# The cross-attention queries of a two-layer encoder: head 0's raw weights loaded with the first sum, later sums loaded later, two tiles for A22's loads

## The chip, the cores and the metric

One core of a Trainium2 chip runs the whole kernel. The metric is the device time of one execution in microseconds (us), as the median of several runs.

## The reference

A two-layer encoder over 512 positions of width 1024, all in float32. Each layer has a mixer (forgetting and differential attention in layer 0, an mLSTM in layer 1), a cross-attention on a memory of 256 positions, and a gated feed-forward net with a short convolution. Cut to what surrounds the change:

```python
x = x + mixed                       # mixer's output projection: mixed @ w_out
x = x + memory_cross_attention(rms_norm(x, xattn_norm[layer]), rms_norm(mem, mem_norm[layer]),
                               xattn_wq[layer], xattn_wkv[layer], xattn_wo[layer])
x = x + conv_ffn(rms_norm(x, ffn_norm[layer]), ffn_w_up[layer], ...)

def memory_cross_attention(xn, memn, wq, wkv, wo):
    q = split_heads(xn @ wq, XATTN_HEADS)        # 4 heads of 256
    k, v = jnp.split(memn @ wkv, 2, axis=-1)
    ...
    out = jnp.einsum('bhqm,bhmd->bhqd', p.astype(v.dtype), v)
    return merge_heads(out) @ wo
```

The change concerns `xn @ wq`, in both layers.

## The kernel before

Activations are kept transposed: `x[0]` to `x[7]` are eight tiles of 128 of the 1024 channels by 512 positions. A product in float32 is made of three in a faster format (`fp32r`): both operands are split into a high part (a cast on ScalarE, ACT, L285) and a low part (a subtraction on VectorE, DVE, L282), and `mm3` (L291 to L293) issues high by high, high by low and low by high on TensorE (PE).

**Queries by seven products.** The weights of one head of `wq` (1024 by 256) and `xn` are taken as 2 by 2 blocks, and `p_query` forms a head's queries with seven block products in place of eight (`p1`, `q2`, `p5`, `p6`, `q7`, `p3`, `p4`). Of the weights it needs, for each head h:
- `raw`, the first half A11, A12 as it lies in memory (1024 columns); its load is L1197.
- `sa`, sums of both halves: `sum_load` loads a pair of blocks on SyncE's queue (SP, L1165) and adds the second half by an accumulating DMA that GpSimd (POOL) issues (L1166). There are three `sa` buffers.
- `sb`, first S2 = part of `sa` + part of `raw` (L1221, DVE), then S4, made in place from S2 and `raw` (L1232).
- `ra`, A22, loaded by `rest_load` (L1171), in a single buffer: the next head's load is issued once the present one has been split.

Of the activations it needs `xh`, `xl` (the two parts of normalised x, even tiles for `p1`, odd ones for `q2`) and four "forms", combinations of x tiles that `form_steps` makes from pairs of them (ACT L1480, DVE L1486 to L1488, ACT cast L1489 into `kv0` to `kv3` and DVE's subtraction into `kv4` to `kv7`).

**The stage.** The mixer's output projection runs over eight blocks (one for each x tile) of 24 matmuls of 512 columns. Each block's result stays in a PSUM bank (`acc`) until DVE adds it to x (L619); then ACT makes `xh` (L603), DVE `xl` (L604), both add up squares for the norm (L597, L598), and two tiles at a time become a form. Two banks are in turn: block m+2 needs the bank that x m has left, so the block of x4 starts when x2 is out. Meanwhile heads 0 and 1 of the queries are begun with the x tiles that exist. After the projection the queries of heads 0 to 3, the keys' products and the softmax follow. Head 0's `seed` (L1207, ACT) copies p1's result, negated, into an accumulator, before the rest of the head's products.

**What sets the order.** `Plan` takes steps with a priority (`p1_`, `p5_`, ...) and dependencies and decides the order in which PE's work is written; the order on DVE, ACT, SP and POOL is set by a recording layer from the same steps. On each engine instructions then run strictly as they stand, and a load that waits on SP holds up the loads behind it. Tiles come from pools with a fixed number of buffers for a name; a new tile waits for the readers of the one whose buffer it takes. `opened` opens the pool `keys` once the mixer's tiles are done with, and loads sums 0, 1 and 2. `fn` of `xattn` opens the pool of the cross-attention (`mp`), with `pg`, a tile whose bytes belong to operands of the mixer's projection until that has ended.

Of the kernel before, what the change touches and what calls it, by code (L numbers as in the profile page):

```python
# [17 lines left out]
P = 128  # L18
# [218 lines left out]
class Builder:  # L237
# [887 lines left out]
    def p_forms(self, pl, layer, mix, used):  # L1125

        def opened():
            mix.close()
            self.kp = self.keys.enter_context(self.tc.tile_pool(name=f"keys{layer}", bufs=1, side="right", reuse_waits="tile"))
            self.forms, self.sums = [], {}  # L1130
            for tag, n, bufs in (("sa", 1024, 3), ("ra", 512, 1)):
                self.til(self.kp, tag, (P, n), bufs=bufs)
            self.kv = [self.til(self.kp, f"kv{i}", (P, 1024), F32R, bufs=1) for i in range(8)]
            for tag in ("s2", "a22", "s4"):
                self.til(self.kp, tag, (P, 1088), F32R, bufs=1)
            self.til(self.kp, "sb", bufs=2)
            self.pad(self.kp, 128)
            for h in range(3):
                self.sum_load(layer, h)

        def form(k):
            th, tl = self.kv[k], self.kv[4 + k]
            self.forms.append((th, tl))
            f, r = self.til(self.kp, "a22", (P, 1088), bufs=1), self.til(self.kp, "s4", (P, 1088), bufs=1)
            for fn in self.form_steps(k, "xat", layer, f[:, :1024].rearrange("p (a b) -> p a b", a=2), r[:, :1024], th, tl):
                fn[1]()

        last = pl.add(opened, 0, used, 100, order=[self.memnorm])
        for k in range(3):
            last = pl.add(  # L1150
                lambda k=k: form(k), 0, self.xdone[2 * k + 1], 100 + 2 * k + 2, order=[last], chain=(("A", 1.5), ("D", 1.4), ("A", 1.0), ("D", 1.2))
            )
        self.formed = [last]
        self.queries = []
        for h in range(2):
            self.queries.append(self.p_query(pl, layer, h, [last] + [q[1] for q in self.queries]))
            self.queries[h] = self.queries[h], next(self.queries[h])
        self.held = [q[1].st for q in self.queries]
# [8 lines left out]

    def rest_load(self, layer, h):

        self.rest = self.til(self.kp, "ra", bufs=1)  # L1170
        self.nc.sync.dma_start(self.rest[:], self.t["xq"][layer, 2 * h + 1][:, 512:])  # L1171

    def p_query(self, pl, layer, h, order):

        nc = self.nc
        tt_ = nc.vector.tensor_tensor
        st = {}
        a1, a2 = self.t["xq"][layer, 2 * h], self.t["xq"][layer, 2 * h + 1]
# [14 lines left out]
        less = lambda out, a, b: tt_(out=out, in0=a[:, :256], in1=b[:], op=ALU.subtract)  # L1193

        def p1():
            st["raw"] = self.til(self.wp, "raw", (P, 1024), bufs=3)
            nc.sync.dma_start(st["raw"][:], a1)  # L1197
            if h == 0:
                self.rest_load(layer, 0)
            st["f3"] = self.parts(OFF)  # L1200
            self.split(*st["f3"], st["raw"][:])
            st["X"] = self.bank("w")
            product(st["f3"], 0, X(0, 0), "X", True)
# [11 lines left out]
        def kept(n, bank):  # L1215
            st[n] = self.til(mp, "xe", (P, MEM), bufs=4)
            nc.scalar.copy(st[n][:], st[bank][:, :256])

        def p6():
            st["sb"] = self.til(self.kp, "sb", bufs=2)  # L1220
            tt_(out=st["sb"][:], in0=self.sums[h][:, 512:], in1=st["raw"][:, :512], op=ALU.add)  # L1221
            if h == 0:
                self.sum_load(layer, 3)
            wide("s2", st["sb"][:])
            product(st["s2"], 0, T2, "Y", False, range(4 - (h == 0)))

# [3 lines left out]

        def p3():
            tt_(out=st["sb"][:], in0=st["sb"][:], in1=st["raw"][:, 512:], op=ALU.add)  # L1232
            wide("s4", st["sb"][:])
            product(st["s4"], 0, X(1, 1), "R", False)

        def p4():
            wide("a22", self.rest[:])
            if h < 3:
                self.rest_load(layer, h + 1)
            product(st["a22"], 0, T4, "Y", False)  # L1240

        n = 1.42
# [15 lines left out]
        pl, mp, fin, ends = yield sd  # L1258
# [9 lines left out]
        u5 = pl.add(lambda: kept("u5", "R"), 0, [q5], p5_ + 0.5, take=("e",))  # L1268
        u2 = pl.add(lambda: kept("u2", "Y"), 0, [q6], p6_ + 0.5, take=("e",))
# [9 lines left out]
    def xattn(self, layer):  # L1279
        nc, t, tc = self.nc, self.t, self.tc  # L1280
        with tc.tile_pool(name=f"xa{layer}", bufs=1, reuse_waits="tile") as mp:
            self.mp = mp
            pl = Plan(self.plan, [st["banks"][0] for st in [*self.fills, *self.held]], s=2, w=0, e=4, q=2, pt=2, wt=1, hs=2)
# [1 line left out]
            for _ in range(2):  # L1285
                self.til(mp, "hs", (P, 1088))
            self.til(mp, "tmp", (P, MEM))
            self.pad(mp, 2048)
            self.pad(mp, 64)
            for tag in ("qh", "ql"):  # L1290
                self.til(mp, tag, (P, 1024), F32R)
# [1 line left out]
            self.til(mp, "pg", (P, 1088), F32R, bufs=1)  # L1293
            self.til(mp, "xe", (P, MEM), bufs=4)
            self.til(mp, "mx", dtype=F32R)

            def last():
                f, r = self.til(mp, "hs", (P, 1088)), self.til(mp, "hs", (P, 1088))
                self.forms.append((self.kv[3], self.kv[7]))
                for fn in self.form_steps(3, "xat", layer, two(f[:, :1024]), r[:, :1024], *self.forms[3]):  # L1300
                    fn[1]()
# [10 lines left out]
            qs, qe = [None] * 4, [None] * 4  # L1312
# [43 lines left out]
            for h in range(4):  # L1356
                p = 50 + 10 * h
                ke = []
                for m in (2 * h, 2 * h + 1):
# [7 lines left out]
                    if m < 2 * len(self.fills):  # L1367
                        st = self.fills[m // 2]
# [3 lines left out]
                                order=ke[-1:] if m % 2 else (),  # L1372
# [125 lines left out]
    def ffn_steps(self, layer, mp):  # L1498
# [1 line left out]


        nc, t = self.nc, self.t
        sc = Sched(raw=3, h=3, s2=1, s4=1, a22=1, sa=3, sb=2, ra=1, hs=2, c=1, dr=2, u2=1, u5=1, act=10, acc=2, y=2, s=2, w=2)
        add = sc.add
        tt = lambda n: 0.055 + 1.06e-3 * n
        act = lambda n: 0.1 + 0.83e-3 * n
# [11 lines left out]
        def joined(deps, prio, free):  # L1518
            return add("-", 0.0, None, deps, prio, (), free, 0.0)

        RAWS = {"raw": (self.wp, 1024, 3), "dr": (mp, 512, 2), "sa": (self.kp, 1024, 3), "sb": (self.kp, 512, 2), "ra": (self.kp, 512, 1)}

        def raw_tile(st, tag):
            pool, n, bufs = RAWS[tag]
            st[tag] = self.til(pool, tag, (P, n), bufs=bufs)
            return st[tag]
# [81 lines left out]
        act_ = lambda: tuple(self.til(mp, i, dtype=F32R, bufs=10) for i in ("ah", "al"))  # L1608
        self.pad(mp, 64)
        act_()  # L1610
        self.pad(mp, 192)
        formed = []
        hs2 = [mp.tile([P, 2, 514], F32, name=f"hs{layer}{i}") for i in range(2)]
        for h in hs2:
# [657 lines left out]
```

## Time and profile before

| | |
|---|---|
| median of 3 runs | 1472.54 us (1472.54 to 1472.64) |
| profiled execution | 1473.89 us, of which the span of the core's instructions 1471.8 us |
| PE busy | 1445.4 us, 98% of the span, 9019 matmuls |
| DVE, ACT, POOL busy | 1258.1, 931.1, 75.1 us |
| mean granted clock of PE | 0.998 |
| DMA | 190.23 MB in 1471.8 us, mean 129 GB/s |
| queries of layer 0, of layer 1 | about 220 to 312 us, 930 to 1020 us of the span |

Times on a row of a timeline are the start in us from the span's start, then the duration in us, engine, line, operation and operands; in brackets is how long the engine stood idle before it and what ended that. A row of the chain of waits is start, duration and what was done or waited for. A row of windows has, for a stretch of the span, each engine's busy time with its count of instructions, the granted clock (1.00 is full), the share of DMA engines' time and GB/s. A row of DMA issues ends with the us from issue to landing.

### The profile page before, as it was taken

What the parts mean: (1) busy time and instruction counts of PE and PEld (TensorE: products, weight loads), DVE (VectorE), ACT (ScalarE), POOL (GpSimd) and SP (SyncE); (2) the same over time, 40 slices, a digit from 0 to 9 for tenths busy, and PEclk for the clock granted to TensorE, in tenths of its full rate; (3) what the DMA queues carried; (4) which work ended last, traced back from release to release, by engine and by line L of the source; (5) the groups of instructions that cost most, each with busy time, mean ns of one, the idle gap of its engine ahead of it and who ended that gap; (6) DMA issues with size and microseconds to landing.
All of it is one profiled execution on the core that took longest, in us unless ns stands there. A gap on an engine that the chain in (4) does not pass through costs nothing.

```text
span 1471.8 us, 24027 instructions
## 1 busy us (share of the span) xinstructions
PE 1445.4 (98%) x9019; PEld 1281.5 (87%) x9019; DVE 1258.1 (85%) x2284; ACT 931.1 (63%) x1655; POOL 75.1 (5%) x116
## 2 busy tenths in 40 slices
PE   9999999899999999999999999999999999999998
PEld 7888787798889999999888888888988999999987
DVE  7789986866799999999778988796769999999974
ACT  7688665665677665666447665565656765656654
POOL 0001120000000000000000100000000000000000
PEclk9999999999999999999999999999999999999999
DMA  5222336452236665553223331746314566555322
GB/s 198 86 73 72 122 119 196 136 180 101 79 119 172 175 159 165 151 165 83 83 101 103 118 103 65 208 114 186 132 49 129 151 175 177 157 154 162 108 68 76
DMA packets 70627, 190.23 MB, mean 129 GB/s; under 512 B 7520, under 2 KB 7520, under 8 KB 70512
## 3 DMA queue, kind: packets, MB, share of 16 engines
q1 hardware_dynamic: 62304, 161.38, 32.4%
q0 software_dynamic: 7200, 26.22, 10.2%
q8 instruction: 70, 1.15, 0.3%
q10 hardware_dynamic: 1008, 1.12, 0.2%
q14 instruction: 45, 0.37, 0.1%
HBM read 186.56 MB, written 2.13 MB: 128 GB/s over the span
## 4 chain that ended last, share of the span: by engine, by line
PE 75%; DVE 14%; ACT 5%; issue 3%; DMA 3%; POOL 0%; SPq 0%; DVEq 0%; ACTq 0%; POOLq 0%
PE acc L291 13%; PE acc L292 13%; PE acc L293 13%; PE w L293 6%; PE w L291 6%; PE w L292 6%; PE s L293 3%; PE s L291 3%; PE s L292 3%; DVE wl L282 3%; PE acc L352 2%; PE acc L354 2%; PE acc L353 2%; DVE c L1656 1%; DMA raw<-in_xq_dram 1%
## 5 line engine op out<-in xcount | busy, mean ns | idle before, releaser
L282 DVE TENSOR_TENSOR wl<-raw,wh 128x1024 fp32r<-128x1024 f32 (+3 forms) x185 | 218.8, 1183 | 30.8 <-ACT wh L285 27.6
L291 PE MATMUL acc<-xh,wh 128*128 128x256 f32 (+1 forms) x624 | 206.9, 332 | 0.1
L293 PE MATMUL acc<-xh,wl 128*128 128x256 f32 (+1 forms) x624 | 205.8, 330 | 0.2 <-DVE wl L282 0.2
L292 PE MATMUL acc<-xl,wh 128*128 128x256 f32 (+1 forms) x624 | 205.6, 329 | 0.0
L285 ACT CAST wh<-raw 128x1024 fp32r<-128x1024 f32 (+1 forms) x127 | 130.8, 1034 | 87.7 <-PE acc L292 43.7
L1656 DVE SCALAR_TENSOR_TENSOR c<-hs,vec,c 128x512 f32<-128x512 f32 x176 | 128.6, 747 | 7.2 <-ACT c L1649 5.9
L291 PEld LDWEIGHTS acc<-xh,wh 128*128 128x128 f32 x624 | 117.2, 188 | 12.1 <-ACT v L1893 0.6
L293 PEld LDWEIGHTS acc<-xh,wl 128*128 128x128 f32 x624 | 117.2, 188 | 12.1 <-DVE wl L282 0.6
L292 PEld LDWEIGHTS acc<-xl,wh 128*128 128x128 f32 x624 | 117.2, 188 | 11.5
L293 PE MATMUL w<-ah,wl 128*128 128x512 f32 x304 | 119.1, 392 | 0.0
L292 PE MATMUL w<-al,wh 128*128 128x512 f32 x304 | 118.6, 390 | 0.0
L291 PE MATMUL w<-ah,wh 128*128 128x512 f32 x304 | 118.5, 390 | 0.0
L1649 ACT ACTIVATE c<-hs,vec 128x512 f32<-128x512 f32 x88 | 69.2, 813 | 13.2 <-DVE hs L1796 11.7
L282 DVE TENSOR_TENSOR s<-sb,s 128x512 fp32r<-128x512 f32 x100 | 68.6, 686 | 5.5 <-ACT s L285 5.5
L293 PEld LDWEIGHTS w<-ah,wl 128*128 128x128 f32 x304 | 57.1, 188 | 11.9
L282 DVE TENSOR_TENSOR wl<-sa,wh 128x1024 fp32r<-128x1024 f32 x50 | 61.1, 1221 | 5.6 <-ACT wh L1727 3.2
L292 PEld LDWEIGHTS w<-al,wh 128*128 128x128 f32 x304 | 57.1, 188 | 10.0
L1727 ACT CAST wh<-sa 128x1024 fp32r<-128x1024 f32 x42 | 44.1, 1049 | 34.3 <-PE w L292 26.4
L291 PEld LDWEIGHTS w<-ah,wh 128*128 128x128 f32 x304 | 57.1, 188 | 9.8
L619 DVE TENSOR_TENSOR x<-w,x 128x512 f32<-128x512 f32 x72 | 49.5, 688 | 18.1 <-PE w L293 18.0
L1545 ACT CAST wh<-dr 128x512 fp32r<-128x512 f32 x64 | 39.6, 618 | 39.2 <-issue 35.5
L1727 ACT CAST s<-sb 128x512 fp32r<-128x512 f32 x84 | 52.1, 620 | 18.5 <-PE s L293 14.6
(525 smaller groups left out, 4631.0 us busy)
## 6 DMA issues: line engine op xcount, KB each, us to landing
raw<-in_up_dram SPq DMA_DIRECT2D x46, 512.0 KB, 3.2
sa<-in_up_dram SPq DMA_DIRECT2D x42, 512.0 KB, 3.7
sa<-in_up_dram POOLq DMA_DIRECT2D x42, 512.0 KB, 5.2
dr<-in_down_dram SPq DMA_DIRECT2D x64, 256.0 KB, 2.9
ra<-in_up_dram SPq DMA_DIRECT2D x42, 256.0 KB, 3.2
raw<-in_xk_dram SPq DMA_DIRECT2D x16, 512.0 KB, 3.4
raw<-in_wo_dram SPq DMA_DIRECT2D x16, 512.0 KB, 3.3
raw<-in_xv_dram SPq DMA_DIRECT2D x16, 512.0 KB, 3.3
```

The costliest lines, as they stand in the source:

```text
L282: self.nc.vector.tensor_tensor(out=lo, in0=v, in1=hi.bitcast(F32), op=ALU.subtract)
L285: self.nc.scalar.copy(hi, v)
L291: mm(out, wh, xh, start=first, stop=False, skip_group_check=parts)
L292: mm(out, wh, xl, start=False, stop=False, skip_group_check=parts)
L293: mm(out, wl, xh, start=False, stop=last, skip_group_check=parts)
L352: mm(ps, xh[k][:, ts], wh[:, ws], start=(k == 0), stop=False)
L353: mm(ps, xh[k][:, ts], wl[:, ws], start=False, stop=False)
L619: self.nc.vector.tensor_tensor(out=self.x[m][:], in0=ps[:], in1=self.x[m][:], op=ALU.add)
L1545: nc.scalar.copy(st["wh"][:, :cols], st[tag][:, :cols])
L1649: nc.scalar.activation(st["c_"][:, j, :], hs()[:, j, 2:514], AF.Identity, scale=self.col("cw", (layer * 3 + 2) * 44 + blk), bias=self.col( ...
L1656: nc.vector.scalar_tensor_tensor(out=c, in0=hs()[:, j, n : n + 512], scalar=w, in1=c, op0=ALU.mult, op1=ALU.add)
L1727: nc.scalar.copy(s["wh"][:, :cols], raw())
```

## The change

Five edits, in both layers:
1. `ra` has two buffers; `rest_load` of head h+2 is issued after head h's A22 has been split (before: of head h+1).
2. `opened` loads sum 0, then head 0's raw weights, into the second of the three `sa` buffers (`self.first`), then head 0's A22. Sum 1 is a step of the plan just behind. Sum 2 is loaded in `p6` of head 0, sum 3 in `p3` of head 0; each takes an `sa` buffer that was read.
3. Head 2's raw weights go to `pg` instead of a `raw` buffer.
4. `sb` of heads 1 and 3 is a tile `qs` of the cross-attention's pool; a pad of 2048 bytes there goes.
5. The feed-forward stage has two `ra` buffers too, in its planner (`Sched`) and its table of tiles; a pad of 192 goes.

```diff
-            for tag, n, bufs in (("sa", 1024, 3), ("ra", 512, 1)):
+            for tag, n, bufs in (("sa", 1024, 3), ("ra", 512, 2)):
...
-            for h in range(3):
-                self.sum_load(layer, h)
+            self.rests = []
+            self.sum_load(layer, 0)
+            self.first = self.til(self.kp, "sa", (P, 1024), bufs=3)
+            self.nc.sync.dma_start(self.first[:], self.t["xq"][layer, 0])
+            self.rest_load(layer, 0)
...
         last = pl.add(opened, 0, used, 100, order=[self.memnorm])
+        pl.add(lambda: self.sum_load(layer, 1), 0, self.xdone[2], 103, order=[last])
...
     def rest_load(self, layer, h):
-        self.rest = self.til(self.kp, "ra", bufs=1)
-        self.nc.sync.dma_start(self.rest[:], self.t["xq"][layer, 2 * h + 1][:, 512:])
+        self.rests.append(self.til(self.kp, "ra", bufs=2))
+        self.nc.sync.dma_start(self.rests[h][:], self.t["xq"][layer, 2 * h + 1][:, 512:])
...
         def p1():
-            st["raw"] = self.til(self.wp, "raw", (P, 1024), bufs=3)
-            nc.sync.dma_start(st["raw"][:], a1)
             if h == 0:
-                self.rest_load(layer, 0)
+                st["raw"] = self.first
+            else:
+                st["raw"] = self.til(mp, "pg", (P, 1088), bufs=1)[:, :1024] if h == 2 else self.til(self.wp, "raw", (P, 1024), bufs=3)
+                nc.sync.dma_start(st["raw"][:], a1)
+            if h == 1:
+                self.rest_load(layer, 1)
...
         def p6():
-            st["sb"] = self.til(self.kp, "sb", bufs=2)
+            st["sb"] = self.til(mp, "qs", bufs=1) if h % 2 else self.til(self.kp, "sb", bufs=2)
...
             if h == 0:
-                self.sum_load(layer, 3)
+                self.sum_load(layer, 2)
...
         def p3():
             tt_(out=st["sb"][:], in0=st["sb"][:], in1=st["raw"][:, 512:], op=ALU.add)
+            if h == 0:
+                self.sum_load(layer, 3)
...
         def p4():
-            wide("a22", self.rest[:])
-            if h < 3:
-                self.rest_load(layer, h + 1)
+            wide("a22", self.rests[h][:])
+            if h < 2:
+                self.rest_load(layer, h + 2)
...
-            self.pad(mp, 2048)
...
+            self.til(mp, "qs", bufs=1)
...
-        sc = Sched(raw=3, ..., ra=1, hs=2, ...)
+        sc = Sched(raw=3, ..., ra=2, hs=2, ...)
...
-        RAWS = {..., "ra": (self.kp, 512, 1)}
+        RAWS = {..., "ra": (self.kp, 512, 2)}
...
-        self.pad(mp, 192)
```

PE's and POOL's instructions stand in the same order as before. Three places on the other engines, all of layer 0, are shown (layer 1 has the first and the last alike). Line numbers after the change are up to 9 higher: L1221 becomes L1228, L1165 L1169, L1171 L1175, L1197 L1204, L1486 L1495. The numbers at names tell tiles of one name apart.

SP's queue from the opening of the pool on, before:

```order
L1165 DMA sa_2665<-in_xq_dram 128x2x512
L1165 DMA sa_2668<-in_xq_dram 128x2x512
L1165 DMA sa_2671<-in_xq_dram 128x2x512
L277 DMA raw_2863<-in_wo_dram 128x1024
L277 DMA raw_2912<-in_wo_dram 128x1024
L1171 DMA ra_2954<-in_xq_dram 128x512
L1197 DMA raw_2952<-in_xq_dram 128x1024
L1197 DMA raw_2982<-in_xq_dram 128x1024
L1197 DMA raw_3259<-in_xq_dram 128x1024
L1197 DMA raw_3380<-in_xq_dram 128x1024
L1171 DMA ra_3188<-in_xq_dram 128x512
L1165 DMA sa_3061<-in_xq_dram 128x2x512
```

The same stretch after the change:

```order
L1169 DMA sa_2665<-in_xq_dram 128x2x512
L1141 DMA sa_2668<-in_xq_dram 128x1024
L1175 DMA ra_2670<-in_xq_dram 128x512
L1169 DMA sa_2798<-in_xq_dram 128x2x512
L277 DMA raw_2864<-in_wo_dram 128x1024
L277 DMA raw_2913<-in_wo_dram 128x1024
L1175 DMA ra_2981<-in_xq_dram 128x512
L1204 DMA raw_2979<-in_xq_dram 128x1024
L1204 DMA raw_3380<-in_xq_dram 128x1024
L277 DMA raw_3515<-in_xv_dram 128x1024
L1169 DMA sa_3060<-in_xq_dram 128x2x512
L1204 DMA pg_3261<-in_xq_dram 128x1024
```

Head 0's raw weights (`sa_2668`) are now the second load; sum 1 (`sa_2798`) still stands ahead of the projection's weights (`wo`), sum 2 (`sa_3060`) and head 2's raw (`pg`) behind the raw loads of heads 1 and 3.

DVE between the steps of the first form (`s`, from x0 and x1) and the evacuation of x4 (`x_142`), before:

```order
L1487 TENSOR_TENSOR s_554_2726<-a_553_2725,s_554_2726 128x256
L619 TENSOR_TENSOR x_140<-acc_549_2691,x_140 128x512
L1488 TENSOR_TENSOR s_554_2726<-a_553_2725,s_554_2726 128x256
L282 TENSOR_TENSOR wl_2825<-raw_2823,wh_2824 128x1024
L604 SCALAR_TENSOR_TENSOR xl_560_2748<-x_140,vec,xh_559_2747 128x512
L282 TENSOR_TENSOR kv_531_2656<-s_554_2726,kv_527_2652 128x1024
L598 TENSOR_TENSOR sq_2683<-sq_2683,sqt_2751 128x512
L619 TENSOR_TENSOR x_141<-acc_558_2740,x_141 128x512
L1221 TENSOR_TENSOR sb_3059<-sa_2665,raw_2952 128x512
L282 TENSOR_TENSOR wl_2865<-raw_2863,wh_2864 128x1024
```

After the change:

```order
L1228 TENSOR_TENSOR sb_3058<-sa_2665,sa_2668 128x512
L619 TENSOR_TENSOR x_140<-acc_549_2689,x_140 128x512
L1496 TENSOR_TENSOR s_554_2724<-a_553_2723,s_554_2724 128x256
L282 TENSOR_TENSOR wl_2826<-raw_2824,wh_2825 128x1024
L1497 TENSOR_TENSOR s_554_2724<-a_553_2723,s_554_2724 128x256
L604 SCALAR_TENSOR_TENSOR xl_560_2746<-x_140,vec,xh_559_2745 128x512
L598 TENSOR_TENSOR sq_2681<-sq_2681,sqt_2749 128x512
L282 TENSOR_TENSOR kv_531_2656<-s_554_2724,kv_527_2652 128x1024
L282 TENSOR_TENSOR s_626_3063<-sb_3058,s_626_3063 128x512
L619 TENSOR_TENSOR x_141<-acc_558_2738,x_141 128x512
```

Head 0's S2 (`sb`) stood behind the evacuation of x3 (`x_141`) and stands now ahead of that of x2 (`x_140`).

DVE around the evacuation of x7 (`x_145`) and the last form (`hs`), after the change:

```order
L619 TENSOR_TENSOR x_145<-acc_591_2919,x_145 128x512
L1228 TENSOR_TENSOR qs_3148<-sa_2798,raw_2979 128x512
L282 TENSOR_TENSOR wl_3045<-sa_2665,wh_3044 128x1024
L604 SCALAR_TENSOR_TENSOR xl_600_2973<-x_145,vec,xh_599_2972 128x512
L598 TENSOR_TENSOR sq_2681<-sq_2681,sqt_2976 128x512
L1495 TENSOR_TENSOR hs_3036<-hs_3035 128x512
L1228 TENSOR_TENSOR sb_3301<-sa_3060,pg_3261 128x512
L1496 TENSOR_TENSOR hs_3036<-hs_3035,hs_3036 128x256
```

The S2s of head 1 (`qs`) and head 2 (`sb`) stood ahead of the evacuations of x5 and x7 and stand now behind that of x7, head 2's between the steps of the last form. On ACT, head 2's A22 (`a<-ra`) stood behind the cast of head 1's queries (`qh<-hs`) and stands now ahead of it; head 2's seed follows both.

More of the change, by code (lines that the diff above doesn't have):

```diff
@@ L1502, in ffn_steps @@
         nc, t = self.nc, self.t
-        sc = Sched(raw=3, h=3, s2=1, s4=1, a22=1, sa=3, sb=2, ra=1, hs=2, c=1, dr=2, u2=1, u5=1, act=10, acc=2, y=2, s=2, w=2)
+        sc = Sched(raw=3, h=3, s2=1, s4=1, a22=1, sa=3, sb=2, ra=2, hs=2, c=1, dr=2, u2=1, u5=1, act=10, acc=2, y=2, s=2, w=2)
         add = sc.add
@@ L1519, in joined @@
             return add("-", 0.0, None, deps, prio, (), free, 0.0)
-        RAWS = {"raw": (self.wp, 1024, 3), "dr": (mp, 512, 2), "sa": (self.kp, 1024, 3), "sb": (self.kp, 512, 2), "ra": (self.kp, 512, 1)}
+        RAWS = {"raw": (self.wp, 1024, 3), "dr": (mp, 512, 2), "sa": (self.kp, 1024, 3), "sb": (self.kp, 512, 2), "ra": (self.kp, 512, 2)}
         def raw_tile(st, tag):
```

## Prediction

> **What bounds the kernel now.** The profile page comes first:
>
> ```profile
> span 1471.8 us, 24027 instructions
> PE 1445.4 (98%) x9019; PEld 1281.5 (87%) x9019; DVE 1258.1 (85%) x2284; ACT 931.1 (63%) x1655; POOL 75.1 (5%) x116
> ```
>
> TensorE is busy for 98% of the span, so a change that leaves its 9019 matmuls alone can win only its idle time, 1471.8 - 1445.4 = 26.4 us, and time at a low clock. So I cut the span into windows of 10 us and looked at those in which the queries are formed (layer 0, then layer 1), for the ones under 10 us of PE:
>
> ```profile
> 250.00:260.00 10.00, 8.29 (x37) 6.58 (x36) 10.00 (x16) 5.61 (x8) 0.00 (x0) 1.00 0.28 97
> 260.00:270.00 10.00, 7.16 (x45) 6.17 (x44) 9.41 (x14) 7.42 (x12) 0.00 (x0) 1.00 0.18 66
> 290.00:300.00 10.00, 7.47 (x64) 7.27 (x63) 5.48 (x7) 4.91 (x9) 0.86 (x1) 1.00 0.51 126
> 1002.60:1006.10 3.50, 3.50 (x19) 3.50 (x19) 1.39 (x2) 1.33 (x3) 0.00 (x0) 0.51 0.47 128
> ```
>
> The columns after the length are PE, PEld, DVE, ACT and POOL busy, then the granted clock, DMA share and GB/s. The last row is a stretch in which PE looks full and runs at 0.51 of its clock. PE's timeline gives each hole with the instruction waited for:
>
> ```profile
> 250.20 0.39 PE L293 MATMUL acc<-qa,wl 128*128 128x512 f32 x1
> 252.30 0.47 PE L291 MATMUL acc<-mh,wh 128*128 128x512 f32 x1 [1.71 <-DVE x L619]
> 257.85 0.39 PE L291 MATMUL acc<-mh,wh 128*128 128x512 f32 x1
> 265.34 0.39 PE L292 MATMUL w<-xl,wh 128*128 128x256 f32 x1 [0.72 <-DVE xl L604]
> 269.38 0.39 PE L291 MATMUL w<-xh,wh 128*128 128x256 f32 x1 [2.12 <-ACT acc L1207]
> 293.59 0.39 PE L291 MATMUL acc<-kv,s 128*128 128x256 f32 x1 [2.53 <-ACT acc L1207]
> 977.65 0.38 PE L291 MATMUL w<-xh,wh 128*128 128x256 f32 x1 [0.84 <-ACT acc L1207]
> 1001.41 0.39 PE L291 MATMUL acc<-kv,s 128*128 128x256 f32 x1 [2.09 <-ACT acc L1207]
> ```
>
> The chain of waits, asked for layer 0's stage, says what stands behind them, and the timelines of VectorE and ScalarE show how:
>
> ```profile
> 236.51 9.73 DMA raw<-in_xq_dram
> 286.25 6.37 DMA ra<-in_xq_dram
> ```
>
> ```profile
> 234.33 0.69 DVE L619 TENSOR_TENSOR x<-acc,x 128x512 f32<-128x512 f32 x1
> 246.32 0.69 DVE L1221 TENSOR_TENSOR sb<-sa,raw 128x512 f32<-128x512 f32 x1 [5.88 <-DMA raw<-in_xq_dram]
> 251.47 0.68 DVE L619 TENSOR_TENSOR x<-acc,x 128x512 f32<-128x512 f32 x1
> 252.07 0.42 DVE L1488 TENSOR_TENSOR s<-a,s 128x256 f32<-128x256 f32 x1
> 252.41 1.22 DVE L282 TENSOR_TENSOR wl<-raw,wh 128x1024 fp32r<-128x1024 f32 x1
> 253.54 0.74 DVE L604 SCALAR_TENSOR_TENSOR xl<-x,vec,xh 128x512 fp32r<-128x512 f32 x1
> 254.20 1.22 DVE L282 TENSOR_TENSOR kv<-s,kv 128x1024 fp32r<-128x1024 f32 x1
> ...
> 267.61 0.69 DVE L619 TENSOR_TENSOR x<-acc,x 128x512 f32<-128x512 f32 x1
> 268.96 0.36 ACT L1207 ACTIVATE acc<-w 128x256 f32<-128x256 f32 x1
> 288.78 1.05 ACT L285 CAST qh<-hs 128x1024 fp32r<-128x1024 f32 x1
> 292.64 0.62 ACT L285 CAST a<-ra 128x512 fp32r<-128x512 f32 x1 [2.81 <-DMA ra<-in_xq_dram]
> ```
>
> The L619 rows take x2, x4 and x7 (output tiles of the mixer's projection) out of their banks. Behind x3's and ahead of x4's DVE stands 5.88 us in front of head 0's S2, whose raw weights were issued only at 236.51. From there it is late with every tile: x4's evacuation ends at 252.15, where PE's next block waits; x6's low half and x7's evacuation (with head 0's seed behind it on ACT) make the holes at 265.34 and 269.38. The hole at 293.59 has its own cause: ACT waits for head 2's A22, issued at 286.25 because the single `ra` was still being read, and the seed stands behind that cast. Layer 1 repeats both more mildly.
>
> **Layer 0, first stall.** Head 0's raw weights are now issued with the first sum and the wait for them goes. What is late next? S2 also reads sum 0, whose accumulation POOL issues. Its rows, and landings of the accumulations as the DMA view gives them for stretches that hold one issue (at 228.87, 230.12, 231.59, 273.90):
>
> ```profile
> 228.87 1.00 POOL L1166 DMA_DIRECT2D sa<-in_xq_dram  x1 [13.34 <-DVE x L619]
> sa<-in_xq_dram POOLq DMA_DIRECT2D x1, 512.0 KB, 8.4
> sa<-in_xq_dram POOLq DMA_DIRECT2D x1, 512.0 KB, 11.6
> sa<-in_xq_dram POOLq DMA_DIRECT2D x1, 512.0 KB, 13.4
> sa<-in_xq_dram POOLq DMA_DIRECT2D x1, 512.0 KB, 5.1
> ```
>
> Sum 0 lands at 228.87 + 8.4 = 237.3, or, if alone in the queues, at 234.0. I take 237.3: before, 1.5 MB of sums are loaded ahead of it and two wo loads follow; now 1.75 MB (two sums, raw, A22), but two accumulations rather than three. DVE reaches S2's new place, ahead of x2's evacuation, at 234.0 and now waits there for about 3.3 us: the stall moves, and is shorter by 2.6. Whether it costs anything is set by when PE needs the banks. A block is 24 matmuls, 257.85 - 252.30 less 0.1 of restart = 5.45 us. Its last matmul of the earlier block starts at 250.20, so without the hole the next block starts at 250.43, and the ones before it start at 244.98 and 239.53: by these, x4, x3 and x2 have to be out. Now the replay, with DVE's pitch from start to start, as the run from 251.47 to 254.20 has it (0.60 for 512 columns, 0.34 for 256, 1.13 for 1024, 0.66 for a low half):
> - S2 237.3 to 237.9; x2 out at 238.6, 0.9 ahead of its need.
> - seven instructions (0.34 + 1.13 + 0.34 + 0.66 + 0.60 + 1.13 + 0.60 = 4.80), then x3: out at 244.0, 1.0 ahead.
> - 1.13 + 0.66 + three of 0.60 + two of 0.34 = 4.27, then x4: out at 248.9, 1.5 ahead. **The hole of 1.71 closes.**
> - From here DVE keeps up: x6's block ends at 255.88, its evacuation is out by 257.6 and its low half by 261.1. PE needs that 1.18 after the start of the query block at 261.33, at 262.5. **0.72 closes.**
> - x7's block ends at 261.33. DVE still has six instructions of 4.7 us between x6 and x7, with an ACT wait of some 0.5 among them, so x7 goes out at 263.5 (the S2 of head 1, which stood in front, moves behind it). ACT's xh (0.63) and the seed (0.36) follow: ready at 264.6. Without holes, PE is there at 264.1 to 264.3 (261.33 plus the 2.9 us of work before the hole). I leave 0.5: **2.12 becomes 0.5.**
>
> **What moves behind.** Head 2's S2 now stands among the steps of the last form, in front of its low half; it needs sum 2 and the raw tile in `pg`. PE's first reader of that half is here:
>
> ```profile
> 275.91 0.28 PE L292 MATMUL s<-kv,wh 128*128 128x256 f32 x1
> ```
>
> In the new time that is 275.91 - 1.71 - 0.72 - 1.6 - some 0.4 of restarts, 271.4. DVE's replay finishes the half at 271.1, if S2 does not wait: it is reached at about 267.2. `pg` is issued when the last product of the projection has read its bytes (about 261.6) and lands 3.3 to 5 us later. Sum 2 follows the split of head 0's raw (about 257.8): 3.7 to 5.2 of load and 5.1 alone to 8.4 beside others, 266.6 to 271.4. Queries move little else over DMA then (0.18 of DMA share at 260:270), so I take the lower end: no wait. The upper end would cost 4 us.
>
> **Layer 0, second stall.** With two `ra` buffers, head 2's A22 is issued after head 0's split, some 20 us earlier. ACT's wait of 2.81 goes, and the seed stands behind the cast of qh: 288.78 + 0.95 + 0.62 + 0.36 is within 290.7, and PE wants it at 293.59 - 2.53 = 291.06. **2.53 closes**, with 0.4 to spare.
>
> **Layer 1.**
>
> ```profile
> 937.54 0.88 POOL L1166 DMA_DIRECT2D sa<-in_xq_dram  x1 [35.20 <-DMA sa<-in_xq_dram]
> sa<-in_xq_dram POOLq DMA_DIRECT2D x1, 512.0 KB, 7.6
> 946.55 0.42 DVE L1487 TENSOR_TENSOR s<-a,s 128x256 f32<-128x256 f32 x1
> 954.60 0.69 DVE L1221 TENSOR_TENSOR sb<-sa,raw 128x512 f32<-128x512 f32 x1 [1.64 <-DMA raw<-in_xq_dram]
> ```
>
> Sum 0 lands at 937.54 + 7.6 = 945.1, and DVE reaches S2 at 946.5: no stall, 1.64 goes, and x7 no longer waits behind two S2s (1.2). That is more than the hole at 977.65: **0.84 closes**; **2.09** as in layer 0. Then the clock: right behind the hole at 1001.41 PE runs 3.50 us at 0.51, a loss of 3.50 x 0.49 = **1.7**. Two holes of layer 0, 2.12 and 2.53 long, had no such stretch behind them (the rows of 260:270 and 290:300 show 1.00). I count 1.7 as gained, since its hole goes. [...]
>
> **Other edits.** Splits, adds and loads are as many as before; each head's `sb` lies elsewhere at the same size. In the feed-forward stage `ra` gets a second buffer too. What the instructions that read or write `ra` waited for, in the whole kernel, ends in few things:
>
> ```profile
> PE acc L293: 25.5, 32
> DMA ra<-in_xq_dram: 5.2, 2
> ```
>
> The only DMA among them is that of the queries (2.81 + 2.37 are its 5.2); no load of the feed-forward stage's `ra` was ever waited for, so an earlier one gains nothing there, and a loss would first have to use up its lead. Taken at 0, from nothing to 1 us of loss.
>
> **Sum.** Layer 0: 1.71 + 0.72 + 1.6 + 2.53 = 6.6. Layer 1: 0.84 + 2.09 + 1.7 = 4.6. Together 11.2. The profiled execution took 1473.89 us, 1.35 above the median of the three runs, 1472.54. So 1473.89 - 11.2 = 1462.7 in profile terms, 1461.3 as a median.
>
> **The rivals.**
> - **Sum 0 lands later than 238.2 (0.17).** Then x2 is out too late, and each further us is PE's. For: raw and A22 now stand in SP's queue beside it, and the second and third accumulations took 11.6 and 13.4. Against: it is the first of two, no longer of three. At 11.6 it lands at 240.5 and costs 2.3, 1463.6; at 13.4, 242.3 and 4.1, 1465.4. [...]
> - **Half clock stays or comes elsewhere (0.09).** For: two like holes went without one, so where it strikes hangs on more than length. Against: no hole above 0.5 should be left. 1463.0.
> - **Slower: sum 2 in front of the last form (0.08).** If its accumulation is as slow as 13.4, sum 2 lands at 276 and PE stands 9 us for the last form, in both layers if layer 1 is alike: 18 lost against 11.2, 1479. It decides against the change from about 5.6 us of wait per layer on, a landing near 273. For: it is now the only sum that is loaded after a wait on DVE. Against: DMA is nearly idle there.
> - **Little change (0.08).** PE arrives 6 us early at the loads of memory values and first feed-forward weights, and waits there for what it no longer waits for here; SP issues several of these by when buffers come free, which comes earlier too. 1466 to 1473; taken as 1470.
>
> **How the numbers follow.** The forecast has 0.58, its own range 1459.0 (the 0.5 gone, some 1.2 of restarts and small holes with it) to 1463. A measurement of this kernel tells about 0.2%, 2.9 us, from no change: faster is below 1469.6, slower above 1475.5. Faster: 0.58 + 0.17 + 0.09 and a little of the last rival, 0.85; same 0.07; slower 0.08. The range reaches over the first two rivals and their sum, 1458.5 to 1468.0.
>
> **What would show it.** Right: PE's holes near 252, 265, 293 and 1001 gone, one of up to 0.5 at head 0's seed, S2 of head 0 waiting about 3 us for POOL's sum before x2, no 0.5 clock near 1000. Wrong: a hole where PE's block waits for x2 (sum 0), one at the last form's readers near 271 (sum 2), or new holes past 300.

## The result and the profile after

The changed kernel took 1461.59 us (median of four, 1460.51 to 1462.36) against 1472.59 us before. The ratio is 0.9923, 95% interval 0.9906 to 0.994. Forecast were 1461.3 us and a range of 1458.5 to 1468.0. The profiled execution took 1460.51 us. One later execution of the changed kernel took 2919.96 us, about twice the others, and is left out of every comparison. The first lines of the profile page:

```profile
span 1458.2 us, 24038 instructions
PE 1441.9 (99%) x9019; PEld 1279.6 (88%) x9019; DVE 1258.1 (86%) x2284; ACT 930.4 (64%) x1655; POOL 74.8 (5%) x116
```

PE has as many matmuls and DVE as much busy time as before; PE's idle time fell from 26.4 to 16.3 us. The windows of 10 us in which the holes stood, and the one with the half clock, are full now. (The columns are those of the prediction's windows; head 2's product, which stood behind the hole at 293.59, lies in 280:290 now.)

```profile
250.00:260.00 10.00, 10.00 (x46) 8.29 (x45) 8.87 (x13) 6.99 (x10) 0.85 (x1) 1.00 0.34 77
260.00:270.00 10.00, 10.00 (x82) 9.64 (x81) 8.96 (x17) 5.52 (x9) 0.86 (x1) 1.00 0.61 168
280.00:290.00 10.00, 10.00 (x90) 10.00 (x90) 8.10 (x12) 7.24 (x13) 0.86 (x1) 1.00 0.74 164
990.00:1000.00 10.00, 10.00 (x89) 10.00 (x88) 6.30 (x9) 5.98 (x11) 1.17 (x2) 1.00 0.83 243
1000.00:1010.00 10.00, 10.00 (x72) 9.02 (x71) 6.92 (x13) 6.82 (x13) 0.56 (x1) 1.00 0.70 176
```

Of VectorE's timeline in layer 0 these are the rows of head 0's S2 (now L1228, `sb<-sa,sa`), of the evacuations of x2 to x7 (L619), of head 2's S2 (`sb<-sa,pg`) and of the last form's low half; the rows between them are left out:

```profile
234.12 0.69 DVE L1228 TENSOR_TENSOR sb<-sa,sa 128x512 f32<-128x512 f32 x1 [0.47 <-DMA sa<-in_xq_dram]
234.73 0.69 DVE L619 TENSOR_TENSOR x<-acc,x 128x512 f32<-128x512 f32 x1
240.14 0.68 DVE L619 TENSOR_TENSOR x<-acc,x 128x512 f32<-128x512 f32 x1
245.14 0.68 DVE L619 TENSOR_TENSOR x<-acc,x 128x512 f32<-128x512 f32 x1
250.32 0.69 DVE L619 TENSOR_TENSOR x<-acc,x 128x512 f32<-128x512 f32 x1 [0.95 <-PE acc L293]
255.76 0.69 DVE L619 TENSOR_TENSOR x<-acc,x 128x512 f32<-128x512 f32 x1 [0.57 <-PE acc L293]
261.20 0.69 DVE L619 TENSOR_TENSOR x<-acc,x 128x512 f32<-128x512 f32 x1
...
265.41 0.69 DVE L1228 TENSOR_TENSOR sb<-sa,pg 128x512 f32<-128x512 f32 x1
...
268.21 1.23 DVE L282 TENSOR_TENSOR kv<-hs,kv 128x1024 fp32r<-128x1024 f32 x1 [0.78 <-ACT kv L1498]
```

The wait of 5.88 us for raw weights has become a wait of 0.47 for sum 0. For x5 and x6 DVE waits for PE, where before PE waited for DVE. POOL issued sum 0's accumulation here, and the DMA view of that stretch gives its landing:

```profile
228.52 1.00 POOL L1170 DMA_DIRECT2D sa<-in_xq_dram  x1 [13.30 <-PE acc L293]
sa<-in_xq_dram POOLq DMA_DIRECT2D x1, 512.0 KB, 5.6
```

It took 5.6 us, not 8.4. Head 2's S2 reads sum 2, whose accumulation was issued at 256.8, and the raw tile in `pg`, issued at 261.0; their landings by the DMA view:

```profile
sa<-in_xq_dram POOLq DMA_DIRECT2D x1, 512.0 KB, 5.8
pg<-in_xq_dram SPq DMA_DIRECT2D x1, 512.0 KB, 3.4
```

Where the time was won shows in the starts of matmuls that both programs have, on PE's timeline. Before:

```profile
228.53 0.50 PE L291 MATMUL acc<-mh,wh 128*128 128x512 f32 x1 [0.33 <-DVE x L619]
277.35 0.38 PE L291 MATMUL s<-xh,s 128*128 128x256 f32 x1 [0.32 <-ACT xe L1217]
435.18 0.39 PE L291 MATMUL acc<-kv,a 128*128 128x256 f32 x1 [0.35 <-DVE hs L1773]
703.40 0.39 PE L291 MATMUL acc<-kv,a 128*128 128x256 f32 x1 [0.24 <-DVE hs L1773]
1144.24 0.39 PE L291 MATMUL acc<-kv,a 128*128 128x256 f32 x1 [0.35 <-DVE hs L1773]
```

and after:

```profile
228.21 0.50 PE L291 MATMUL acc<-mh,wh 128*128 128x512 f32 x1 [0.32 <-DVE x L619]
271.44 0.39 PE L291 MATMUL s<-xh,s 128*128 128x256 f32 x1 [0.31 <-ACT xe L1224]
426.67 0.39 PE L291 MATMUL acc<-kv,a 128*128 128x256 f32 x1 [0.35 <-DVE hs L1781]
694.82 0.39 PE L291 MATMUL acc<-kv,a 128*128 128x256 f32 x1 [0.24 <-DVE hs L1781]
1130.72 0.38 PE L291 MATMUL acc<-kv,a 128*128 128x256 f32 x1 [0.35 <-DVE hs L1781]
```

The lead of the changed kernel is 0.3 us where the stage begins, 5.9 behind head 0's products, 8.5 and 8.6 early and late in layer 0's feed-forward stage, and 13.5 early in layer 1's. So in these two executions layer 0's queries gave 8.2 us, layer 1's 4.9, and the feed-forward stage nothing. The profiled executions differ by 13.4 us and the medians by 11.0: the one of before lies 1.3 above its median and this one 1.1 below.

### The profile page after: what moved, and what is told of

Read it like the earlier page. It is cut to its first block, busy times and chain, and to the rows that moved or that the text cites. A ratio compares the mean times of both kernels' runs of the same rounds, so it can differ in the third digit from the quotient of the medians.

```text
span 1458.2 us, 24038 instructions
## 1 busy us (share of the span) xinstructions
PE 1441.9 (99%) x9019; PEld 1279.6 (88%) x9019; DVE 1258.1 (86%) x2284; ACT 930.4 (64%) x1655; POOL 74.8 (5%) x116
## 4 chain that ended last, share of the span: by engine, by line
PE 74%; DVE 17%; ACT 4%; issue 3%; DMA 1%; POOL 0%; SPq 0%; DVEq 0%; ACTq 0%; POOLq 0%
PE acc L291 14%; PE acc L292 14%; PE acc L293 14%; PE w L291 5%; PE w L293 5%; PE w L292 5%; DVE wl L282 3%; DVE c L1664 3%; PE s L291 3%; PE s L293 3%; PE s L292 3%; PE acc L352 2%; PE acc L354 2%; PE acc L353 2%; DVE hs L1804 1%
## 5 line engine op out<-in xcount | busy, mean ns | idle before, releaser
L282 DVE TENSOR_TENSOR wl<-raw,wh 128x1024 fp32r<-128x1024 f32 (+3 forms) x181 | 214.4, 1185 | 31.2 <-ACT wh L285 28.1
L285 ACT CAST wh<-raw 128x1024 fp32r<-128x1024 f32 (+1 forms) x123 | 126.5, 1033 | 89.3 <-PE acc L292 46.8
L292 PEld LDWEIGHTS acc<-xl,wh 128*128 128x128 f32 x624 | 117.3, 188 | 11.6
L1657 ACT ACTIVATE c<-hs,vec 128x512 f32<-128x512 f32 x88 | 69.3, 813 | 13.4 <-DVE hs L1804 11.8
L619 DVE TENSOR_TENSOR x<-w,x 128x512 f32<-128x512 f32 x72 | 50.1, 696 | 18.0 <-PE w L293 17.8
L282 DVE TENSOR_TENSOR s<-sb,s 128x512 fp32r<-128x512 f32 x92 | 63.7, 692 | 0.3 <-ACT s L285 0.3
```

Source lines behind the costliest of these rows:

```text
L282: self.nc.vector.tensor_tensor(out=lo, in0=v, in1=hi.bitcast(F32), op=ALU.subtract)
L285: self.nc.scalar.copy(hi, v)
L292: mm(out, wh, xl, start=False, stop=False, skip_group_check=parts)
L619: self.nc.vector.tensor_tensor(out=self.x[m][:], in0=ps[:], in1=self.x[m][:], op=ALU.add)
L1657: nc.scalar.activation(st["c_"][:, j, :], hs()[:, j, 2:514], AF.Identity, scale=self.col("cw", (layer * 3 + 2) * 44 + blk), bias=self.col( ...
```

## The experiments

The theory is that each of PE's holes has its own cause, A22's single buffer or DVE's backlog behind a stalled S2, and that the wait of a moved S2 costs PE nothing until an evacuation or a seed behind it is late. The rivals are these: holes overlap and hide one another; the stage goes at the pace of sum 0's accumulation; the feed-forward edit has a part; and, for the half clock, that it belongs to one place.

**The changed kernel again.** No edit.

> The changed kernel again, on the chip of the next three runs, as their yardstick. All theories: 1461.6, between 1460.5 and 1462.4 as its earlier runs; PE has no hole over 0.5 us between 228 and 310 us and between 930 and 1010 us, and no stretch at half clock in the two query stages.

1460.55 us, ratio to before 0.9925 (0.9912 to 0.9937). But this execution has a hole, as DVE's and PE's timelines show:

```profile
236.78 0.69 DVE L1228 TENSOR_TENSOR sb<-sa,sa 128x512 f32<-128x512 f32 x1 [3.73 <-DMA sa<-in_xq_dram]
264.15 0.39 PE L291 MATMUL w<-xh,wh 128*128 128x256 f32 x1 [0.72 <-ACT acc L1214]
```

POOL issued the accumulation at 228.58, so it was 8.2 us on its way. Here the replay of the prediction (landing 8.4, stall 3.3, hole 0.5) came about nearly as written; in the first profile it did not. The expectation of no hole over 0.5 was a miss.

**The second A22 buffer alone**, on the kernel before (shown in part; the load of head 1's A22 and the feed-forward stage's planner and table change as in the whole change):

```diff
-            for tag, n, bufs in (("sa", 1024, 3), ("ra", 512, 1)):
+            for tag, n, bufs in (("sa", 1024, 3), ("ra", 512, 2)):
...
-            if h < 3:
-                self.rest_load(layer, h + 1)
+            if h < 2:
+                self.rest_load(layer, h + 2)
```

> The kernel before with the second A22 buffer alone (queries and feed-forward stage; the rest of head h+2 loaded after head h's split); head 0's raw weights come as late as before. Theory (each hole has its own cause, and the gains add): the holes of 2.53 and 2.09 us in front of head 2's product go, the half clock of 1.7 with the second, the holes of 1.71, 0.72, 2.12 and 0.84 stay: 6.3 us less than before, 1466.3. Rival 1 (the late raw weights are the one cause, and A22 would be waited for elsewhere): within 1 us of before. Rival 2 (the holes overlap: a stage that is late by the first stall hides A22's gain, or the other way round): 2 to 4 us less, and then the sum of this and the next run's gains is not that of the whole change.

1466.36 us, 4.9 less than the 1471.23 of the kernel before on the same chip; ratio 0.9963 (0.9949 to 0.9977). That lies between the theory's 6.3 and the 2 to 4 of the second rival. Head 2's two holes are gone; of the others 1.94, 1.49 and 0.39 us stay (ahead of x6's block, at head 0's seed in layer 0 and in layer 1). A half clock followed the hole ahead of x6's block, where no earlier profile had one, and the hole of 0.72 did not open, since PE came later to x6's low half. PE's timeline, then a window:

```profile
251.91 0.52 PE L291 MATMUL acc<-mh,wh 128*128 128x512 f32 x1 [1.94 <-DVE x L619]
252.20:255.50 3.30, 3.30 (x9) 2.60 (x8) 3.30 (x4) 3.30 (x5) 0.00 (x0) 0.50 0.30 118
```

**One A22 buffer, the rest of the change kept** (shown in part, as above):

```diff
-            for tag, n, bufs in (("sa", 1024, 3), ("ra", 512, 2)):
+            for tag, n, bufs in (("sa", 1024, 3), ("ra", 512, 1)):
...
-            if h < 2:
-                self.rest_load(layer, h + 2)
+            if h < 3:
+                self.rest_load(layer, h + 1)
```

> The changed kernel with one A22 buffer, as before (queries and feed-forward stage), all else of the change kept. Theory (gains add): the holes in front of head 2's product come back in both layers, about 2.5 and 2.1 us, at new times: 4.6 to 6.3 us slower than the changed kernel, 1466.2 to 1467.9, the difference being whether half clock follows a hole. Rival on the clock (half clock belongs to a hole over 2 us in that place): a stretch of 3.4 us at 0.5 behind the hole of layer 1, as before. [...]

1463.53 us, 3.0 more than the changed kernel on the same chip and less than the 4.6 to 6.3 expected. Both holes came back, smaller, and no half clock followed either: the window shown, that of layer 1, has a clock of 1.00, and the mean clock of the execution is 0.999, where the four profiled with a half clock have 0.998:

```profile
287.44 0.39 PE L291 MATMUL acc<-kv,s 128*128 128x256 f32 x1 [1.85 <-ACT acc L1212]
994.11 0.39 PE L291 MATMUL acc<-kv,s 128*128 128x256 f32 x1 [2.03 <-ACT acc L1212]
990.00:1005.00 15.00, 12.97 (x112) 12.78 (x111) 9.01 (x12) 8.13 (x15) 1.58 (x2) 1.00 0.63 169
```

Alone, A22's buffer gave 4.9 us and the rest of the change 7.7 (1463.53 against 1471.23); together 12.6, where the whole gave 10.7. The intervals are 1.8 to 2.1 us to either side, so the sum neither shows an overlap nor excludes one. Each part closes its own holes. Where the two may overlap is the half clock: the mean granted clocks of these runs are 0.9976 before, 0.9988 with either part and 0.9992 with both, so either part alone takes most of it away. That would be some 1.3 of the 1.9 us, an estimate from clocks that are given to 0.001.

**The feed-forward stage planned for one buffer:**

```diff
-        sc = Sched(raw=3, ..., ra=2, hs=2, ...)
+        sc = Sched(raw=3, ..., ra=1, hs=2, ...)
```

> The changed kernel with the feed-forward stage planned for one A22 buffer as before (the tiles stay two); only two pairs of ACT instructions change places, one in each layer. Theory: 0, within 0.3 us of the changed kernel. Rival (the part of the gain that the query stages don't show comes from there): 0.5 to 1.5 us slower.

1460.42 us, 0.1 from the changed kernel: the order that this edit gives the feed-forward stage is worth nothing, as expected.

**Sum 0 loaded last** (raw, A22, sum 1, sum 0):

```diff
-            self.sum_load(layer, 0)
             self.first = self.til(self.kp, "sa", (P, 1024), bufs=3)
             self.nc.sync.dma_start(self.first[:], self.t["xq"][layer, 0])
             self.rest_load(layer, 0)
+            self.sum_load(layer, 1)
+            self.sum_load(layer, 0)
...
-        pl.add(lambda: self.sum_load(layer, 1), 0, self.xdone[2], 103, order=[last])
```

> The changed kernel with the four first loads in another order: head 0's raw, A22, sum 1, then sum 0. DVE's order follows: head 0's S2 stands one tile later, ahead of x3's evacuation (about 239.3) and no longer ahead of x2's. Theory (the wait for sum 0's accumulation costs nothing as long as each x tile is out before PE's block needs its bank): sum 0 is accumulated from about 231.7 on and lands at 237 to 240.5, S2 waits 0 to 1.5 us, x3 is out by 242 against a need of 244.7: the same time as the changed kernel or up to 0.5 us less, since the hole of 0.7 at head 0's seed that a stall of 3.7 left in one profile can't come. Rival (sum 0's accumulation is the pace of the stage): every us of its later landing is seen on PE, 2 to 5 us slower.

1462.77 us, ratio 0.9945 (0.9931 to 0.9959), slower than the changed kernel's 0.9923 to 0.9927 by about 0.2%, with intervals that overlap. Expected was the same or faster: a miss. Sum 0's accumulation was issued at 233.24, 1.2 us behind sum 1's, and took 9.9 us by the DMA view. DVE and PE:

```profile
243.21 0.69 DVE L1228 TENSOR_TENSOR sb<-sa,sa 128x512 f32<-128x512 f32 x1 [5.12 <-DMA sa<-in_xq_dram]
244.64 0.47 PE L291 MATMUL acc<-mh,wh 128*128 128x512 f32 x1 [0.30 <-ACT s L285]
265.65 0.38 PE L291 MATMUL w<-xh,wh 128*128 128x256 f32 x1 [1.55 <-ACT acc L1214]
```

x3 went out at 244.5, just late, and DVE's backlog reached head 0's seed. The stall of 5.12 us left holes of 1.85 us together, so PE does not lose a us for every us that sum 0 is late, as the rival has it.

**Head 2's raw weights in the ring:**

```diff
-                st["raw"] = self.til(mp, "pg", (P, 1088), bufs=1)[:, :1024] if h == 2 else self.til(self.wp, "raw", (P, 1024), bufs=3)
+                st["raw"] = self.til(self.wp, "raw", (P, 1024), bufs=3)
```

> The changed kernel with head 2's raw weights in the ring of raw buffers, as before the change, in place of the other pool's tile. On DVE head 2's S2 moves from the steps of the last form to ahead of x7's evacuation. It needs sum 2, whose accumulation is issued at about 257 to 258 and in the changed kernel has landed by 265.4. Theory (a wait on DVE ahead of a tile's evacuation is what costs): x7, ready at about 261.2, waits until sum 2 has landed, 262.5 to 266; head 0's seed comes 1 to 4.5 us later and PE has a hole of that length less 0.2 there, in both layers: 1.5 to 8 us slower than the changed kernel. Rival (where the S2s of heads 1 and 2 stand is of no account, the early raw weights of head 0 are all): within 0.5 us of the changed kernel.

> Head 2's raw weights in the ring of raw buffers once more, beside the changed kernel on one chip. Theory (its S2 ahead of x7's evacuation waits for sum 2 by as much as the first run showed, 0.7 and 0.9 us): holes of 0.3 to 0.5 at head 0's seed in both layers, 0.6 to 1.2 us slower than the changed kernel in all. Rival (the two holes are chance): within 0.3 us.

The first time 1462.88 us (ratio 0.9947, 0.9931 to 0.9963), with holes of 0.29 and 0.44. The second time 1464.12 against 1461.21 for five executions of the changed kernel on the same chip, 2.9 slower, more than the 0.6 to 1.2 expected; the ratios are 0.9944 (0.9926 to 0.9962) and 0.9927 (0.9909 to 0.9946), but the fastest of the six (1462.66) is slower than the slowest of the five (1462.48). The second profile, which is of the slowest of the six (DVE, PE, a window):

```profile
237.68 0.69 DVE L1228 TENSOR_TENSOR sb<-sa,sa 128x512 f32<-128x512 f32 x1 [4.58 <-DMA sa<-in_xq_dram]
264.97 0.69 DVE L1228 TENSOR_TENSOR sb<-sa,raw 128x512 f32<-128x512 f32 x1 [1.59 <-DMA sa<-in_xq_dram]
239.12 0.47 PE L291 MATMUL acc<-mh,wh 128*128 128x512 f32 x1 [0.24 <-ACT s L285]
267.35 0.58 PE L291 MATMUL w<-xh,wh 128*128 128x256 f32 x1 [3.31 <-ACT acc L1214]
267.60:270.60 3.00, 3.00 (x15) 3.00 (x16) 3.00 (x7) 1.12 (x3) 0.00 (x0) 0.52 0.47 170
```

The second L1228 row is head 2's S2, ahead of x7's evacuation and waiting for sum 2. Two stalls in one execution leave a hole of 3.31, and a half clock follows it. Of the two, only the 1.59 us belongs to this edit; the 4.58 is sum 0's, which was 8.6 us on its way here. So where the later S2s stand does count, and the tile in `pg`, which lets head 2's stand behind x7, is a part of the gain.

**S2 of heads 1 and 3 in the old buffers:**

```diff
-            st["sb"] = self.til(mp, "qs", bufs=1) if h % 2 else self.til(self.kp, "sb", bufs=2)
+            st["sb"] = self.til(self.kp, "sb", bufs=2)
```

> The changed kernel with S2 and S4 of heads 1 and 3 in the two old buffers in place of the new tile. On DVE head 1's S2 moves ahead of x4's evacuation, one instruction of 0.6 us, where the changed kernel's DVE is 1.5 us or more ahead. Its raw weights land at about 240 to 243 and sum 1 at about 239 to 241. Theory: 0 to 0.3 us. Rival (head 1's S2 ahead of an evacuation waits as head 0's did before): raw at 243 stalls DVE at about 243.5 by no more than 1 us, and the hole at head 0's seed grows to 0.7 to 1.5 us.

1462.11 us, ratio 0.9941 (0.9927 to 0.9956). The profile had a stall of 3.69 for sum 0, as in the first run above (3.73, hole 0.72), and this on PE:

```profile
264.51 0.39 PE L291 MATMUL w<-xh,wh 128*128 128x256 f32 x1 [1.21 <-ACT acc L1214]
```

That is 0.5 more, about the one instruction that now stands ahead of x4. It did not wait; it is only work ahead of the seed. The difference in time is inside the intervals.

**Sum 1 second:**

```diff
             self.sum_load(layer, 0)
+            self.sum_load(layer, 1)
             self.first = self.til(self.kp, "sa", (P, 1024), bufs=3)
...
-        pl.add(lambda: self.sum_load(layer, 1), 0, self.xdone[2], 103, order=[last])
```

> The changed kernel with sum 1 loaded directly behind sum 0, ahead of head 0's raw and A22; all other engines keep their order. Then sum 1's accumulation is issued about 1.3 to 2 us behind sum 0's, not 3.1. Theory (the accumulations and the loads share the DMA engines, and sum 0's takes 8 us and more when they meet): sum 0 lands 8.4 to 9.5 us after issue, near 237.5, S2 waits 4 to 5 us, x2 is out at about 238.8 and in time, x7 and head 0's seed are 0.7 to 1.5 us late: 0.4 to 1 us slower than the changed kernel. Rival (what makes the accumulation 5.6 or 8.2 us is chance, not company): no difference in time, landing anywhere between 5 and 8.5. Second rival (raw, now third, lands after the sum): S2 waits for raw, at 235 or before.

1462.59 us, ratio 0.9942 (0.9928 to 0.9956). Sum 0's accumulation was issued at 229.73, with sum 1's 1.2 us behind, and took 8.9 us:

```profile
238.70 0.69 DVE L1228 TENSOR_TENSOR sb<-sa,sa 128x512 f32<-128x512 f32 x1 [5.35 <-DMA sa<-in_xq_dram]
240.14 0.47 PE L291 MATMUL acc<-mh,wh 128*128 128x512 f32 x1 [1.05 <-ACT s L285]
266.09 0.38 PE L291 MATMUL w<-xh,wh 128*128 128x256 f32 x1 [1.08 <-ACT acc L1214]
```

Here x2 was late, and the block of x4 waited 1.05 us for it. (The row names a cast on ACT, which had the same S2 to wait for; the bank is freed by x2's evacuation, which ended at 240.) This is the first rival of the prediction, brought about by the order of the loads.

The profile counts the packets of loads and of accumulations on the same 16 DMA engines: in 215:300 of the kernel before, 36.6% of the engines' time for the queue of the loads and 20.8% for that of the accumulations. Whether sum 1's accumulation is the reason for the 8.9 us is not shown. In the kernel before and in the run with the second A22 buffer alone the next accumulation was issued 1.2 to 1.3 us behind sum 0's as well, and sum 0's took 8.4 and 7.5 us. The rows of the second of these:

```profile
229.45 1.00 POOL L1166 DMA_DIRECT2D sa<-in_xq_dram  x1 [14.57 <-DMA sa<-in_xq_dram]
230.67 0.86 POOL L1166 DMA_DIRECT2D sa<-in_xq_dram  x1 [0.22 <-issue]
sa<-in_xq_dram POOLq DMA_DIRECT2D x1, 512.0 KB, 7.5
```

**Head 0's A22 later:**

```diff
-            self.rest_load(layer, 0)
...
-            if h == 1:
-                self.rest_load(layer, 1)
+            if h < 2:
+                self.rest_load(layer, h)
```

> The changed kernel with head 0's A22 loaded behind the projection's last weights, as before, so that sum 1 is the third load: a dose between the changed kernel (sum 1's accumulation issued 3.1 us behind sum 0's) and the run with sum 1 second (1.2). Theory of company: issued 2 to 2.7 us behind, sum 0 lands 7 to 9 us after issue, S2 waits 3 to 5 us, 0.2 to 1 us slower than the changed kernel. Rival (bytes in front are what counts, and 256 KB fewer are): sum 0 lands 0.5 us sooner, same time or 0.3 us faster.

1462.63 us, ratio 0.9932 (0.9914 to 0.9951) against 0.9927 (0.9909 to 0.9946) for the changed kernel: no difference that the runs can tell. Sum 0 took 8.1 us, S2 waited 3.58, the hole was 0.62. The changed kernel's three profiles had 5.6, 8.2 and 6.7 us, and the four runs above that leave its first loads as they are had 7.2, 5.4, 8.6 and 8.1. So this run decides between neither theory. Over all profiles sum 0's accumulation took 5.4 to 8.6 us where the next was issued 2.5 us or more behind it (ten executions), and 7.5, 8.4 and 8.9 where it was 1.2: a close companion may cost something, but the ranges overlap. The 9.9 us of the run with sum 0 last stand beside 10.0 to 11.6 for the other accumulations that were issued second, 1.2 us behind the first.

**The changed kernel on that chip**, and **another execution of the kernel before**, no edits:

> The changed kernel a third time, as the yardstick of the next two runs. 1460.5 to 1461.6. Head 0's S2 waits 0.4 to 3.8 us for sum 0, and PE's hole at head 0's seed goes with it: none up to a wait of some 2.6 us, 0.7 at 3.7.

> The kernel before, another execution looked at. All: PE's holes within 0.4 us of 1.71, 0.72, 2.12, 2.53, 0.84 and 2.09. [...]

The changed kernel: S2 waited 1.98, no hole over 0.5 in either stage. The kernel before (1472.18 us), PE's timeline and two windows:

```profile
268.48 0.38 PE L291 MATMUL w<-xh,wh 128*128 128x256 f32 x1 [2.16 <-ACT acc L1207]
270.00:271.00 1.00, 1.00 (x6) 1.00 (x6) 1.00 (x4) 0.00 (x0) 0.00 (x0) 0.50 0.73 264
271.00:272.00 1.00, 1.00 (x7) 1.00 (x7) 0.73 (x3) 0.23 (x1) 0.00 (x0) 0.50 0.61 234
1000.63 0.39 PE L291 MATMUL acc<-kv,s 128*128 128x256 f32 x1 [1.83 <-ACT acc L1207]
```

The half clock is in layer 0 this time, behind head 0's seed, and not near 1001. So it does not belong to one place. The holes of this execution also came out up to 1 us from those of the first profile (0.76 where 1.71 was, 1.71 where 2.53 was), more than expected; the six add up to 7.8 us, where those of the first add up to 10.0.

## Why the prediction was right

- **The holes.** 1.71, 0.72, 2.53, 0.84 and 2.09 closed as said; of 2.12, 0.5 was to be left, and the changed kernel's profiles show 0, 0.72 and 0. The mechanism, a DVE that is late from 246 to 268 us behind one stalled instruction, is shown by what brings holes back. Over the profiles a wait of head 0's S2 of up to 2.65 us leaves none; 3.6 to 3.7 leave 0.6 to 0.7 (1.2 with head 1's S2 ahead of the seed too); 5.1 to 5.4 leave 1.9 to 2.1. No run loads head 0's raw weights early and leaves the sums and the S2s where they were, so the shares of these edits in the 7.7 us are not measured one by one.
- **Sum 0's landing** was the term mis-sized in the first profile: 5.6 us for 8.4, so the stall was 0.47 and not 3.3. It cost nothing because the cover of 0.9 us ahead of x2 was right. The later execution with 8.2 gave stall and hole within 0.4 of the replay. The value taken is near the upper end of what this DMA does from execution to execution, 5.4 to 8.6.
- **The point at which it costs**, a landing after 238.2, held: at 238.7, in an execution that ran 0.6 us ahead of the one in which 238.2 was worked out, the block waited 1.05 us; at 237.7, in one that ran 0.9 ahead, it waited 0.24.
- **The last form.** Head 2's S2 was reached at 265.4 and did not wait. By the DMA view sum 2, issued at 256.8, took 5.8 us, and the raw tile in `pg`, issued at 261.0, took 3.4. So the rival of a slower kernel was 2.8 us away from a first wait for sum 2, and `pg` landed 1.0 us ahead, within the 0.6 to 2.3 of the prediction's replay; so `pg`, not sum 2, was the nearer one. The reason given for a quick sum 2, that DMA is nearly idle there, did not hold: the share at 260:270 is 0.61 now, for 0.18 before.
- **A22.** Head 2's seed ended at 284.6 without a hole; its price by itself was 4.9 and 3.0 us by two routes, for 6.3 in the sum. This term was read from one execution; in the other execution of the kernel before the two holes are 1.71 and 1.83, for 2.53 and 2.09, and no half clock follows them (1.00 at 990:1005; the mean clock is 0.998, as in the first, which also has one stretch).
- **The clock.** The 1.7 us were credited to the hole at 1001. The runs show a half clock, in no fixed place, behind holes of 2.09 us (for about 3.4 us by windows of 0.2 us: 0.68 at 1002.6, 0.50 on to 1006.0, 0.79 there), 1.94 (0.50 over the 3.30 us shown), 2.16 (0.50 over the 2 us shown) and 3.31 (0.52 over the 3.00 us shown), and none behind others of 1.71, 2.12 and 2.53 (1.00 in the prediction's windows) and of 2.03 (1.00 in the window above). What decides between them is not shown. Closing the holes takes away the occasion, so the amount was about right and the reason was not. Both profiles of before have one such stretch, but the mean clock differs between executions: of the 33 beside the experiments, the six with a mean granted clock of 0.996 took 1475.0 us on average and the seven with 0.999 took 1469.2. The changed kernel has 0.999 or 1.000 in all 15. The means of the clocks (0.9976 and 0.9991) make the gain some 2.2 us, an estimate.
- **Restarts.** The sum left out that each of the six holes cost PE 0.25 to 0.27 us more than its bracket, by the starts of its matmuls (250.43 expected, 252.30 started and its second matmul 0.08 late again, for a bracket of 1.71). Six holes make 1.6 us. With the 0.5 that was not left standing, this is nearly all of the 2.2 us by which the two profiles differ more than the sum.
- **Luck.** That the median came within 0.3 us of the forecast is in part luck. Layer 0 gave 8.2 us for 6.6 and layer 1 4.9 for 4.6, and the profile 1460.5 for 1462.7. The sum was too small by the restarts and too large for a median, since it was read from an execution with 10.0 us of holes, where the other has 7.8; these two errors, of about 2 us each, cancel.

What stays open is how much of the scatter of an accumulation's landing (5.6 to 8.2 us in one program) is company on the DMA engines and how much chance. None of the variants is faster than the changed kernel beyond the scatter.

## What to carry to other kernels

Where an engine works through its instructions in order, look at what stands behind a stalled instruction, and for how long the backlog lasts: here one load issued late made three holes on another engine over 17 us. Moving the stall ahead, where the next consumer has slack, can be as good as removing it (here a stall of up to 2.65 us left no hole), up to a point that can be worked out from the consumer's block times. A gain counted from one execution's holes should allow for DMA landings that differ by 3 us between executions (5.4 to 8.6 here), and a half clock should be booked as a chance on every hole of about 2 us (1.94 drew one here, 2.03 and 2.53 did not), not on one place.

## What was not expected of the hardware

One 512 KB accumulating DMA, in the same place of the same program, took 5.6, 6.7 and 8.2 us in three executions, and 5.4 to 8.6 with the runs that leave the first loads as they are. With the next accumulation issued 1.2 to 1.3 us behind it, it took 7.5, 8.4 and 8.9. The half clock followed a hole of 1.94 us and passed by one of 2.53.
